# Ten of twelve modulation vectors as row dot products on VectorE in place of fp32 products on TensorE, in a two-layer trunk step

## The chip, the cores and the metric

One NeuronCore of a Trainium2 chip runs the whole kernel; nothing is shared with other cores. The metric is the device time of one execution in microseconds. Before the change three runs gave 2442.68, 2445.26 and 2446.33 us, median 2445.26. The kernel is fp32 in and out: its large products are split into float32r parts that TensorE takes at full rate, three products for one.

## What is computed

One inference step of a two-layer trunk with D = 1024, on 512 sample tokens and 128 prompt tokens. Each token group has a conditioning vector (`c` and `c_ctx`), and each layer turns it into six modulation vectors with one linear map:

```python
def trunk_layer(x, cond, l, P, rope, ctx):
    mod = (jax.nn.silu(cond) @ P['w_mod'][l] + P['b_mod'][l])[:, None, :]
    sh1, sc1, g1, sh2, sc2, g2 = jnp.split(mod, 6, axis=-1)
    h = rmsnorm(x) * (1.0 + sc1) + sh1
    mix, ctx_out = token_mixer(h, l, P, rope, ctx)
    x = x + g1 * mix
    h = rmsnorm(x) * (1.0 + sc2) + sh2
    u = dwconv3(h @ P['w_up'][l], P['ffn_conv_w'][l], P['ffn_conv_b'][l])
    x = x + g2 * ((jax.nn.silu(u[..., :D_FF]) * u[..., D_FF:]) @ P['w_down'][l])
    return x, ctx_out
```

`token_mixer` runs one input projection whose columns feed three branches: a chunked spatial-gating MLP, a chunkwise mLSTM and a differential attention. Each is projected to 1024 columns, multiplied by its sigmoid gate and summed, and one output projection follows. `w_mod` is [2, 1024, 6144] in fp32. The two groups of tokens share all weights and differ in the modulation vectors, so the vectors are needed for two conditionings. Two layers and six vectors make the twelve of the title.

## The kernel before

Features lie on the 128 partitions, tokens on the free axis: an activation is eight tiles of 128x640. A product with a 128-column tile of weights has eight steps of k, three terms each (high by high, high by low, low by high) and two halves of 320 tokens, 48 matmuls of line 129. The weights for it come as one chunk of 128x1024 (512 KB) through the tag `raw`, a ring of three slots in SBUF. `weights` (lines 90 to 103) loads a chunk and splits it: ScalarE writes the high part of 512 columns (line 100), VectorE and GpSimd in turns subtract it for the low part (line 101). All transfers of the kernel are issued by SP, in one order, and a transfer that needs a slot waits for those who still read that slot; the transfers behind it wait too. `acc` and `ms` are the PSUM accumulators, two of each.

A tile scheduler sets the order on each engine when the kernel is built. It works through the program with a model of the engines, and what results is a fixed sequence for each engine with semaphore waits between them; `keep_in_program_order` pins single instructions, `high_priority` moves a piece forward.

A layer runs like this: the spatial gating, the mLSTM's and the attention's heads, with the output tiles of the branches between the heads (`branch`: for each output tile m a gate product of 48 matmuls, then a half product of 24 with `w_branch`, then an accumulation by VectorE in line 897 or 899), last the attention branch, whose first five gates are made ahead (`AHEAD`). Then come `w_out` and, in `handoff`, the next norm: the last two tiles of a product and the first two of the next are cut into token halves, so that VectorE and ScalarE norm one half while TensorE works on the other. The FFN (`ffn`) makes two `w_up` tiles for each of 22 f, convolves them on VectorE out of the accumulator (lines 165 and 167), and sums with `w_down` in three parts of f.

Modulation vectors are made in half vectors of 512 columns. `mod_products` (from line 250) loads `w_mod` in eight tiles of 128x512 (line 259), and TensorE multiplies eight times a 32-column stationary `cs`, the silu of the conditionings padded with zeros, by 512 columns of fp32, four products side by side in column groups of the array (line 264). A copy (line 269), four transposes (line 277), a reduction over the four groups (line 281) and the bias (lines 285 and 287) follow. The first two vectors of layer 0 are made in `start` in quarters of 256 columns. `mod_step` does the next half vector of a list: within the attention branch after each output tile but the first, and in the FFN after f = 2 and 4 and after odd tiles of `w_down`. Its tiles have tags of their own (`wk`, `y`, `mw`) and not `raw`.

## Time and profile before

| | |
|---|---|
| median of the runs | 2445.26 us (2442.68 to 2446.33) |
| span of the profiled execution | 2439.1 us |
| what lies around that span, to the median | 6 us |
| granted TensorE clock, mean | 0.998 |
| bytes moved by DMA | 227 MB, 93 GB/s in the mean |

The profile is one execution. Its times count from the start of the span. TensorE (PE) is the busy engine; its weight loads (PEld) run beside the matmuls. DVE is VectorE, ACT ScalarE, POOL GpSimd. SP only issues transfers. The chain of work that ended last is followed back from the last instruction, at each step to what released it or to what ran before it on its engine.

### The profile page before, as it was taken

How to read it: one execution, taken by the hardware profiler on the slowest of the kernel's cores; microseconds unless marked ns; L12 is line 12 of the kernel's file. 1: busy time of each engine (PE TensorE's matmuls, PEld its weight loads, DVE VectorE, ACT ScalarE, POOL GpSimd, SP SyncE). 2: the span in 40 equal slices, each digit the busy share in tenths (PEclk: the TensorE clock that was granted, in tenths of full speed). 3: DMA queues.
4: the chain of work that ended last, by engine and by line, in shares of the span. 5: the costliest groups of instructions: out<-in, count | busy, mean ns of one | idle time of the engine just before them, and what ended most of it. 6: DMA issues, size and time to landing. Idle time of an engine off the chain costs nothing.

```text
span 2439.1 us, 40662 instructions
## 1 busy us (share of the span) xinstructions
PE 2408.0 (99%) x16708; PEld 2313.9 (95%) x16708; DVE 1134.0 (46%) x2111; ACT 944.8 (39%) x1728; POOL 669.9 (27%) x486
## 2 busy tenths in 40 slices
PE   8999999999999999999999999999999999999998
PEld 7999999999598999999999999999986989999998
DVE  5455545553146433424446455455532454244344
ACT  4433335544145322323454332455442543232334
POOL 2322232332222322313213222323322223232231
PEclk9999999999999999999999999999999999999999
DMA  8221221123544234222322212211233432222222
GB/s 282 74 73 64 65 78 62 60 72 132 173 147 160 69 109 140 72 75 79 103 80 70 74 64 66 76 54 62 97 114 120 147 96 74 79 74 73 81 72 69
DMA packets 88761, 227.39 MB, mean 93 GB/s; under 512 B 9472, under 2 KB 23936, under 8 KB 88576
## 3 DMA queue, kind: packets, MB, share of 16 engines
q1 hardware_dynamic: 88576, 224.80, 28.2%
q8 instruction: 131, 2.15, 0.4%
q14 instruction: 54, 0.44, 0.1%
HBM read 217.41 MB, written 7.35 MB: 92 GB/s over the span
## 4 chain that ended last, share of the span: by engine, by line
PE 96%; DVE 3%; ACT 1%; DMA 0%; issue 0%; SPq 0%; DVEq 0%; POOL 0%; POOLq 0%; ACTq 0%
PE acc L129 77%; PE acc L156 6%; PE ms L264 3%; PE ms L869 2%; PE ms L840 2%; PE ms L156 1%; PE ms L862 1%; PE ms L716 1%; PE ms L718 1%; PE ms L705 1%; DVE x L439 0%; PE ms L670 0%; PE ms L536 0%; PE ms L277 0%; PE ms L327 0%
## 5 line engine op out<-in xcount | busy, mean ns | idle before, releaser
L129 PE MATMUL acc<-h,whi 128*128 128x320 f32 x6464 | 1246.9, 311 | 5.0 <-DVE h L356 3.3
L129 PEld LDWEIGHTS acc<-h,whi 128*128 128x128 f32 x6464 | 1019.3, 188 | 32.1 <-issue 19.3
L100 ACT CAST whi<-raw 128x512 fp32r<-128x512 f32 x596 | 365.3, 614 | 1038.1 <-PE acc L129 787.9
L101 POOL TENSOR_TENSOR wlo<-raw,whi 128x512 fp32r<-128x512 f32 (+1 forms) x298 | 390.7, 1311 | 1355.1 <-ACT whi L100 1304.7
L129 PE MATMUL acc<-h,wlo 128*128 128x320 f32 x3232 | 755.4, 310 | 0.0
L129 PEld LDWEIGHTS acc<-h,wlo 128*128 128x128 f32 x3232 | 544.2, 188 | 3.5 <-issue 3.4
L101 DVE TENSOR_TENSOR wlo<-raw,whi 128x512 fp32r<-128x512 f32 (+1 forms) x298 | 241.2, 810 | 451.0 <-ACT whi L100 435.0
L129 PE MATMUL acc<-act,whi 128*128 128x320 f32 x1408 | 269.6, 310 | 0.0
L129 PEld LDWEIGHTS acc<-act,whi 128*128 128x128 f32 x1408 | 222.0, 188 | 4.2 <-issue 2.5
L129 PE MATMUL acc<-act,wlo 128*128 128x320 f32 x704 | 165.5, 309 | 0.0
L129 PE MATMUL acc<-y,whi 128*128 128x320 f32 x768 | 154.3, 314 | 1.7 <-DVE y L114 1.7
L499 DVE SCALAR_TENSOR_TENSOR x<-acc,mod,x 128x128 f32<-128x128 f32 (+3 forms) x136 | 66.3, 527 | 181.3 <-PE acc L129 181.3
L165 DVE SCALAR_TENSOR_TENSOR cw<-acc,vec,cw 128x511 f32<-128x511 f32 (+1 forms) x176 | 95.7, 544 | 115.1 <-ACT cw L163 114.0
L156 PE MATMUL acc<-whi,h 128*128 128x256 f32 x768 | 145.7, 283 | 0.0
L129 PEld LDWEIGHTS acc<-y,whi 128*128 128x128 f32 x768 | 121.2, 188 | 17.3 <-issue 11.7
L156 PEld LDWEIGHTS acc<-whi,h 128*128 128x128 f32 x768 | 123.0, 192 | 0.0
L129 PEld LDWEIGHTS acc<-act,wlo 128*128 128x128 f32 x704 | 119.1, 188 | 0.0
L916 POOL TENSOR_TENSOR cw<-cw,cw 128x640 f32<-128x640 f32 x44 | 69.2, 1573 | 156.5 <-DVE cw L167 151.9
L156 PE MATMUL acc<-wlo,h 128*128 128x256 f32 x384 | 108.7, 283 | 0.0
L167 DVE SCALAR_TENSOR_TENSOR cw<-acc,vec,cw 128x511 f32<-128x511 f32 (+1 forms) x176 | 96.7, 550 | 6.0
L129 PE MATMUL acc<-y,wlo 128*128 128x320 f32 x384 | 92.1, 315 | 0.0
L848 ACT ACTIVATE wk<-ms,mx 128x640 f32<-128x640 f32 (+1 forms) x80 | 56.7, 709 | 76.6 <-DVE mx L846 73.2
(257 smaller groups left out, 2425.0 us busy)
## 6 DMA issues: line engine op xcount, KB each, us to landing
raw<-w_in_f SPq DMA_DIRECT2D x98, 512.0 KB, 3.4
raw<-w_up SPq DMA_DIRECT2D x88, 512.0 KB, 3.3
wk<-w_mod SPq DMA_DIRECT2D x72, 256.0 KB, 3.4
mw<-w_mod SPq DMA_DIRECT2D x72, 256.0 KB, 5.7
raw<-w_down SPq DMA_DIRECT2D x32, 448.0 KB, 3.3
raw<-w_in_v SPq DMA_DIRECT2D x24, 512.0 KB, 3.7
raw<-w_branch SPq DMA_DIRECT2D x24, 512.0 KB, 3.3
mw<-w_mod SPq DMA_DIRECT2D x16, 512.0 KB, 8.8
```

What stands on the lines that cost most here:

```text
L100: nc.scalar.copy(hi, raw[:, a:b])
L101: self.alt().tensor_sub(lo, raw[:, a:b], hi.bitcast(F32))
L129: ins = nc.tensor.matmul(acc[:, s], a[:, sl], b[:, s], start=k == 0 and i == 0, stop=k == last and i == 2)
L156: nc.tensor.matmul(accs[b], a[:, bs], w[:, sl], start=first and b % 2 == 0, stop=last and (b % 2 == 1 or b == NB - 1))
L165: nc.vector.scalar_tensor_tensor(dst[:, a + 1 : b], acc[:, a : b - 1], w0, dst[:, a + 1 : b], ALU.mult, ALU.add)
L167: nc.vector.scalar_tensor_tensor(dst[:, a : b - 1], acc[:, a + 1 : b], w2, dst[:, a : b - 1], ALU.mult, ALU.add)
L264: ins = nc.tensor.matmul(ps[j : j + 32, 0:width], self.cs[:, k, :], raws[k], start=k < 4, stop=k >= 4, tile_position=(0, j))
L499: self.nc.vector.scalar_tensor_tensor(x[:, a:b], acc[:, a:b], g[:, k, i : i + 1], x[:, a:b], ALU.mult, ALU.add)
L840: nc.tensor.matmul(ps[:, s : s + 320], st[:, qs], kk[:, s : s + 320], start=i == 0, stop=i == 1)
L848: nc.scalar.activation(e[:, 0:nk], ps[:, 0:nk], AF.Exp, bias=mx, scale=scale, accum_out=sm[:, j : j + 1])
L869: nc.tensor.matmul(po, at[:, c * P : (c + 1) * P], vv, start=c == 0, stop=c == n - 1)
L916: nc.gpsimd.tensor_mul(cs[0], cs[0], cs[1])
```

## The change

The two vectors that `start` needs at once stay as they are. The other ten are computed as rows of a transposed `w_mod`: the array `w_modT` holds, for each layer and section, 16 blocks of 64 features with 1024 inputs each. `late_consts` now builds `cb`, a 128x1024 tile with silu of `c` on the lower 64 partitions and of `c_ctx` on the upper ones: two transfers that repeat one row on 64 partitions, a tanh on ScalarE, one operation on VectorE. A `mod_step` takes a slot of `raw`, loads the same block of 64 rows twice, once to each half of the partitions (line 306), and lets VectorE multiply it with `cb` and sum along the row (line 307). Sixteen steps make a vector; then four copies of 64x8 bring the sums into the layout that the norms read, and the bias is added. There are 160 steps. `branch` calls two of them after each output tile of all three branches, so 48 a layer; the FFN calls four after each f below 4, two after the others and one after each part, until the list is empty. The sections move with it: 2 is now made in the gating branch's tiles, 3 in the mLSTM's, 4 in the attention's, and 5 with the next layer's 0 and 1 in the FFN.

```diff
+    def conditionings(self, cp):
...
+        self.cb = self.t(cp, [P, D], F32, "cb")
+        for g in range(2):
+            nc.sync.dma_start(self.cb[64 * g : 64 * g + 64, :], I["cB"][g : g + 1].broadcast_to([64, D]))
+        th = self.t(self.wp, [P, D], F32, "raw")
+        nc.scalar.activation(th, self.cb, AF.Tanh, scale=0.5)
+        nc.vector.scalar_tensor_tensor(self.cb, th, 1.0, self.cb, ALU.add, ALU.mult)
...
-    def mod_step(self, src, pin=False):
-        if self.mod_todo:
-            l, sec, n = self.mod_todo.pop(0)
-            self.mod_part(l, sec, 512 * n, 512, src, pin)
+    def mod_step(self):
+        if not self.mod_todo:
+            return
+        nc = self.nc
+        l, sec, k = self.mod_todo.pop(0)
+        if k == 0:
+            self.mod_raw = self.t(self.mp, [P, KD, 2], F32, "modraw", 2)
+        w = self.t(self.wp, [P, D], F32, "raw")
+        for g in range(2):
+            nc.sync.dma_start(w[64 * g : 64 * g + 64, :], self.I["w_modT"][l, sec * 2 * KD + k])
+        nc.vector.scalar_tensor_tensor(w, w, 0.5, self.cb, ALU.mult, ALU.mult,
+                                       accum_out=self.mod_raw[:, k // 2, k % 2 : k % 2 + 1])
+        if k == 2 * KD - 1:
+            m = self.mods[l, sec] = self.t(self.mp, [P, KD, 2], F32, f"mod{sec}", 2)
+            for g in range(2):
+                for i in range(2):
+                    nc.vector.tensor_copy(m[64 * i : 64 * i + 64, :, g], self.mod_raw[64 * g : 64 * g + 64, :, i])
+            c = V_BMOD + sec * KD
+            b = self.vecs[l][:, c : c + KD].unsqueeze(2).to_broadcast([P, KD, 2])
...
     def branch(self, l, n, h, ys, merged, ms, first=False, last=False, ahead=None):
...
             if last:
                 out.append(self.split(merged[m], self.hp, "h", scale=0.5))
-                if m:
-                    self.mod_step((p, "wk", 1), pin=True)
+            self.mod_step()
+            self.mod_step()
...
             for f in range(len(acts), min(f1 + 1, NF)):
                 up(f)
-                if f in (2, 4):
-                    self.mod_step((p2, "mw", 1))
+                for _ in range(4 if f < 4 else 2):
+                    self.mod_step()
+            self.mod_step()
...
-                elif m % 2:
-                    self.mod_step((p2, "mw", 1))
...
-                    self.mod_todo = [(l, s, n) for s in (2, 3, 4) for n in range(2)][1 if l else 0 :]
+                    self.mod_todo = [(l, s, k) for s in (2, 3, 4) for k in range(2 * KD)]
...
-                    self.mod_todo = [(l, 5, 0), (l, 5, 1)]
-                    if nxt:
-                        self.mod_todo += [(l + 1, s, n) for s in (0, 1) for n in range(2)] + [(l + 1, 2, 0)]
+                    self.mod_todo = [(l + s // 6, s % 6, k) for s in ((5, 6, 7) if nxt else (5,)) for k in range(2 * KD)]
```

Three places show how the sequences change. The number behind a tile's name tells tiles of one tag apart; lines after 207 stand some 10 to 30 further down in the changed file.

SP's queue ahead of the attention branch's tiles in layer 0. Before, behind three chunks of `w_branch`: the last two of eight `w_mod` tiles, which go to slots of their own (`wk`), a table, the weights of gates 5 and 6, and the first two of eight more tiles:

```order
L259 DMA wk_6459<-w_mod 128x512
L259 DMA wk_6461<-w_mod 128x512
L224 DMA lc_12635<-rope 128x512
L94 DMA raw_6695<-w_in_f 128x1024
L94 DMA raw_6820<-w_in_f 128x1024
L259 DMA wk_6522<-w_mod 128x512
L259 DMA wk_6524<-w_mod 128x512
```

After the change, from behind the chunk of `w_branch` for output tiles 2 and 3, ahead of which four more steps stand (each `w_modT` row is two transfers, and the `w_in_f` chunks are gates 5 and 6):

```order
L306 DMA raw_6619<-w_modT 64x1024 x2
L306 DMA raw_6623<-w_modT 64x1024 x2
L306 DMA raw_6658<-w_modT 64x1024 x2
L234 DMA lc_12631<-rope 128x512
L306 DMA raw_6662<-w_modT 64x1024 x2
L94 DMA raw_6666<-w_branch 128x1024
L306 DMA raw_6707<-w_modT 64x1024 x2
L306 DMA raw_6711<-w_modT 64x1024 x2
L94 DMA raw_6716<-w_in_f 128x1024
L306 DMA raw_6807<-w_modT 64x1024 x2
L306 DMA raw_6811<-w_modT 64x1024 x2
L94 DMA raw_6816<-w_in_f 128x1024
```

The small tiles have gone, and steps that share the ring with the weights stand between the chunks.

VectorE at that place: the y parts are the attention's outputs (line 114), line 899 is the accumulation of an output tile. Before:

```order
L114 SCALAR_TENSOR_TENSOR y_6342<-acc_6335,gains_543,y_6341 128x640
L281 TENSOR_REDUCE mod_1007_6295<-ms_6312 128x8
L114 SCALAR_TENSOR_TENSOR y_6352<-acc_6345,gains_543,y_6351 128x640
L287 TENSOR_TENSOR mod_1007_6295<-mod_1007_6295,vec_7_90 128x8
L114 SCALAR_TENSOR_TENSOR y_6362<-acc_6355,gains_543,y_6361 128x640
L114 SCALAR_TENSOR_TENSOR y_6372<-acc_6365,gains_543,y_6371 128x640
L899 SCALAR_TENSOR_TENSOR qk_6049<-qk_6049,acc_6385 128x640
L899 SCALAR_TENSOR_TENSOR qk_6110<-qk_6110,acc_6416 128x640
```

After the change, where the accumulation is line 927:

```order
L307 SCALAR_TENSOR_TENSOR raw_6662,modraw_6530<-raw_6662,cb_540 128x1024
L114 SCALAR_TENSOR_TENSOR y_6456<-acc_6449,gains_549,y_6455 128x640
L114 SCALAR_TENSOR_TENSOR y_6466<-acc_6459,gains_549,y_6465 128x640
L307 SCALAR_TENSOR_TENSOR raw_6707,modraw_6530<-raw_6707,cb_540 128x1024
L114 SCALAR_TENSOR_TENSOR y_6476<-acc_6469,gains_549,y_6475 128x640
L307 SCALAR_TENSOR_TENSOR raw_6711,modraw_6530<-raw_6711,cb_540 128x1024
L114 SCALAR_TENSOR_TENSOR y_6486<-acc_6479,gains_549,y_6485 128x640
L307 SCALAR_TENSOR_TENSOR raw_6807,modraw_6530<-raw_6807,cb_540 128x1024
L927 SCALAR_TENSOR_TENSOR qk_6197<-qk_6197,acc_6499 128x640
L307 SCALAR_TENSOR_TENSOR raw_6811,modraw_6530<-raw_6811,cb_540 128x1024
L927 SCALAR_TENSOR_TENSOR qk_6258<-qk_6258,acc_6539 128x640
```

Steps have come between the y parts, and one ahead of each of the two accumulations.

SP's queue at the start of the FFN of layer 0, before, from the first chunk of `w_up`:

```order
L94 DMA raw_7661<-w_up 128x1024
L94 DMA raw_7671<-w_up 128x1024
L94 DMA raw_7848<-w_up 128x1024
L94 DMA raw_7913<-w_up 128x1024
L94 DMA raw_7984<-w_up 128x1024
L259 DMA mw_8425<-w_mod 128x512
```

After:

```order
L94 DMA raw_7679<-w_up 128x1024
L94 DMA raw_7689<-w_up 128x1024
L94 DMA raw_7866<-w_up 128x1024
L94 DMA raw_7931<-w_up 128x1024
L306 DMA raw_8002<-w_modT 64x1024 x2
L306 DMA raw_8006<-w_modT 64x1024 x2
L306 DMA raw_8010<-w_modT 64x1024 x2
L306 DMA raw_8014<-w_modT 64x1024 x2
L94 DMA raw_8019<-w_up 128x1024
L94 DMA raw_8084<-w_up 128x1024
L306 DMA raw_8154<-w_modT 64x1024 x2
```

Four steps follow the first four chunks, and four more the next two; before, sixteen `w_mod` tiles of `mw` stood behind the first five.

ScalarE in `start`, before: the last copies of the column products, the last h tiles, then the gelu's table.

```order
L269 COPY ev_445<-ms_436 128x256
L269 COPY ev_460<-ms_451 128x256
L438 ACTIVATE h_470<-x_112,mod_35_206,mod_30_188 128x512
L438 ACTIVATE h_470<-x_112,mod_35_206,mod_30_188 128x128
L438 ACTIVATE h_477<-x_113,mod_35_206,mod_30_188 128x512
L438 ACTIVATE h_477<-x_113,mod_35_206,mod_30_188 128x128
L506 ACT_TABLE_LOAD
```

After:

```order
L275 COPY ev_445<-ms_436 128x256
L275 COPY ev_460<-ms_451 128x256
L211 ACT_TABLE_LOAD
L211 ACTIVATE raw_543<-cb_540 128x1024
L534 ACT_TABLE_LOAD
L534 ACTIVATE warm_579<-ones_78 128x1
L466 ACTIVATE h_470<-x_112,mod_35_206,mod_30_188 128x512
L466 ACTIVATE h_470<-x_112,mod_35_206,mod_30_188 128x128
```

The tanh of `cb` and two table loads have come ahead of these h tiles.

## Rows read from the trace of the kernel before

**Rows 1.** The page, part 1: engine busy us (share) xinstructions.

```profile
PE 2408.0 (99%) x16708; PEld 2313.9 (95%) x16708; DVE 1134.0 (46%) x2111; ACT 944.8 (39%) x1728; POOL 669.9 (27%) x486
```

**Rows 2.** The page, part 4: the chain that ended last, by engine and by line.

```profile
PE 96%; DVE 3%; ACT 1%; DMA 0%; issue 0%; SPq 0%; DVEq 0%; POOL 0%; POOLq 0%; ACTq 0%
PE acc L129 77%; PE acc L156 6%; PE ms L264 3%; PE ms L869 2%; PE ms L840 2%; PE ms L156 1%; PE ms L862 1%; PE ms L716 1%; PE ms L718 1%; PE ms L705 1%; DVE x L439 0%; PE ms L670 0%; PE ms L536 0%; PE ms L277 0%; PE ms L327 0%
```

**Rows 3.** Line 264 by stretch: from:to, length, PE busy, PEld busy, clock, DMA share, GB/s.

```profile
590.00:680.00 90.00, 29.82 (x96) 4.40 (x96) 1.00 0.45 144
680.00:1300.00 620.00, 18.42 (x112) 3.44 (x112) 1.00 0.32 103
...
1800.00:1870.00 70.00, 25.82 (x80) 3.74 (x80) 1.00 0.39 129
1870.00:2440.00 570.00, 6.34 (x32) 1.10 (x32) 0.99 0.26 85
```

**Rows 4.** The chain from 590 to 680, its last row from 735 to 830: start, us, what.

```profile
by line: PE acc L129 60.9%; PE ms L264 31.2%; PE ms L277 2.4%; DVE y L114 2.0%; ACT y L113 1.8%; PE acc L744 0.9%; ACT modev L269 0.7%; issue 0.2%; PE ms L869 0.1%
...
620.78 0.78 PE acc L129 x4
...
773.19 56.95 PE acc L129 x387
```

**Rows 5.** VectorE's groups by form: busy us, mean ns of one, idle before.

```profile
L854 DVE SCALAR_TENSOR_TENSOR wk<-wk,smx,wk 128x640 f32<-128x640 f32 x32 | 28.9, 904 | 24.8 <-ACT wk L853 24.5
...
L899 DVE SCALAR_TENSOR_TENSOR tg<-tg,acc 128x640 f32<-128x640 f32 x26 | 21.2, 816 | 44.0 <-PE acc L129 43.3 <-issue 0.7
...
L846 DVE TENSOR_SCALAR mx<-mx 128x1 f32<-128x1 f32 x80 | 12.1, 151 | 2.0
```

**Rows 6.** Line 101 (weight splits) on VectorE: ns min/median/max, first and last start.

```profile
L101 DVE TENSOR_TENSOR wlo<-raw,whi x298: 545/692/2054, 20.6 to 2413.0; 128x512 fp32r<-128x512 f32 x141, 128x384 fp32r<-128x384 f32 x8
```

**Rows 7.** The page, part 6: DMA issues, KB each, median us to landing.

```profile
raw<-w_in_f SPq DMA_DIRECT2D x98, 512.0 KB, 3.4
...
wk<-w_mod SPq DMA_DIRECT2D x72, 256.0 KB, 3.4
mw<-w_mod SPq DMA_DIRECT2D x72, 256.0 KB, 5.7
```

**Rows 8.** SP's queue at two stretches, in order of time: start us, us, issues.

```profile
572.69 10.21 SPq L94 DMA_DIRECT2D raw<-w_branch  x2
...
754.71 12.10 SPq L259 DMA_DIRECT2D mw<-w_mod  x16
...
772.34 0.80 SPq L259 DMA_DIRECT2D mw<-w_mod  x2
```

**Rows 9.** VectorE at two stretches, in order of time: start us, us, operation.

```profile
688.02 0.82 DVE L899 SCALAR_TENSOR_TENSOR tg<-tg,acc 128x640 f32<-128x640 f32 x1 [0.70 <-PE acc L129]
...
748.10 0.68 DVE L101 TENSOR_TENSOR wlo<-raw,whi 128x512 fp32r<-128x512 f32 x1
...
769.15 0.75 DVE L165 SCALAR_TENSOR_TENSOR cw<-acc,vec,cw 128x511 f32<-128x511 f32 x1 [1.97 <-ACT cw L163]
```

**Rows 10.** ScalarE at the start, in order of time: start us, us, operation.

```profile
41.49 0.37 ACT L269 COPY ev<-ms 128x256 f32<-128x256 f32 x1 [0.49 <-PE ms L264]
42.98 2.29 ACT L438 ACTIVATE h<-x,mod,mod 128x512 fp32r<-128x512 f32 x4 [1.11 <-DVE mod L287]
45.29 1.28 ACT L506 ACT_TABLE_LOAD   x1
```

**Rows 11.** Line 218, the load of sg_wT: ns, first and last start, us to landing.

```profile
L218 SPq DMA_DIRECT2D lc<-sg_wT x2: 328/380/432, 32.9 to 529.7; - x2
...
DMA to landing us min/median/max: 6.8/6.8/6.8
```

**Rows 12.** All engines by stretch at the start; PEclk is the granted clock.

```profile
10.00:14.00 4.00, 0.26 (x3) 0.07 (x1) 3.58 (x5) 3.52 (x5) 0.00 (x0) 1.00 1.06 386
14.00:18.00 4.00, 3.82 (x24) 3.82 (x25) 0.32 (x2) 0.61 (x2) 0.00 (x0) 0.70 1.08 402
```

More of the change, by code (lines that the diff above doesn't have):

```diff
@@ L179, in consts @@
         nc.vector.memset(self.eps, EPS)
+    def conditionings(self, cp):
+        nc, I = self.nc, self.I
         ct = self.t(cp, [P, KD, 2], F32, "ct")
@@ L244, in lambdas @@
         nc.vector.tensor_scalar(self.lam, s[:, 0:1], s[:, 1:2], self.lam_init, ALU.subtract, ALU.add)
-    def mod_part(self, l, sec, c0, width, src, pin=False):
-        self.mod_vector(*self.mod_products(l, sec, c0, width, src, pin))
     def mod_products(self, l, sec, c0, width, src, pin=False):
@@ L258, in mod_products @@
             r = self.t(pool, [P, per, width], F32, tag)
-            nc.sync.dma_start(r, self.I["w_mod"][l, sec * 2 + c0 // 512, :, k : k + per, c0 % 512 : c0 % 512 + width])
+            nc.sync.dma_start(r, self.I["w_mod0"][sec * 2 + c0 // 512, :, k : k + per, c0 % 512 : c0 % 512 + width])
             raws += [r[:, i, :] for i in range(per)]
@@ L287, in mod_vector @@
             nc.vector.tensor_add(m, m, b)
-    def mod_step(self, src, pin=False):
-        if self.mod_todo:
-            l, sec, n = self.mod_todo.pop(0)
-            self.mod_part(l, sec, 512 * n, 512, src, pin)
+    def mod_step(self):
[17 more added lines that the diff above has]
+            b = self.vecs[l][:, c : c + KD].unsqueeze(2).to_broadcast([P, KD, 2])
+            if sec in (1, 4):
+                nc.vector.scalar_tensor_tensor(m, m, 1.0, b, ALU.add, ALU.add)
+            else:
+                nc.vector.tensor_add(m, m, b)
     def norm_open(self, l, sec, pool, tag):
@@ L384, in start @@
         nc, pin = self.nc, self.tc.keep_in_program_order
+        self.conditionings(p0)
         x = [self.t(p0, [P, NT], F32, "x") for _ in range(KD)]
@@ L981, in run @@
                     with tc.tile_pool(name="p0", bufs=1, reuse_waits="tile") as p0:
-                        h, accs = self.start(Tags(p0, {"x": 8, "mw": 16, "sq": 2, "sqa": 2, "ev": 2}))
+                        h, accs = self.start(Tags(p0, {"x": 8, "mw": 16, "sq": 2, "sqa": 2, "ev": 2, "ct": 1, "cth": 1, "cs": 1}))
                     self.late_consts()
@@ L1012, in run @@
                     ahead = {m: self.gate(l, G_DA, m, h, t) for m, t in enumerate(AHEAD)}
-                    self.mod_step((self.p1, "y", 1), pin=True)
                     ys = self.attn_out(os, dsums)
@@ L1016, in run @@
                 with tc.tile_pool(name=f"p2{l}", bufs=1, reuse_waits="tile") as p2:
-                    tags = Tags(p2, {"x": 8, "cw": 8, "act": 20, "mw": 8, "sq": 2, "sqa": 2})
+                    tags = Tags(p2, {"x": 8, "cw": 8, "act": 20, "sq": 2, "sqa": 2})
                     x = [self.t(tags, [P, NT], F32, "x") for _ in range(KD)]
@@ L1082, in _layout @@
     A["final_g"] = f["final_g"].reshape(KD, P).T
-    A["w_mod"] = f["w_mod"].reshape(L, KD, P, 12, 512).transpose(0, 3, 2, 1, 4)
+    wm = f["w_mod"]
+    A["w_mod0"] = wm[0, :, : 2 * D].reshape(KD, P, 4, 512).transpose(2, 1, 0, 3)
+    A["w_modT"] = wm.transpose(0, 2, 1).reshape(L, 12 * KD, 64, D)
+    A["cB"] = np.stack([f["c"][0], f["c_ctx"]], 0)
     w = f["w_in"]
```

## Prediction

> **What bounds the kernel now.** I read the page first: TensorE is busy 2408.0 of 2439.1 us, VectorE 1134.0, less than half [rows 1]. The chain of work that ended last says the same from the other side: 96% of it is TensorE, 77% the split products of line 129, 3% the modulation products of line 264 [rows 2]. So an operation taken off TensorE shortens the run by its length as long as TensorE's next products are ready, and one put on VectorE costs nothing until TensorE waits for it. Where the modulation products stand is read from their busy time by stretch [rows 3]: four stretches, of which 590 to 680 and 1800 to 1870 (the attention branch of either layer) hold the most. Then I looked into those stretches with the chain [rows 4] and at the places where the change puts its new work: the queue of transfers, VectorE's sequence, ScalarE's at the start.
>
> The measured runs have a median of 2445.3 us and the profiled execution has a span of 2439.1, so I add 6 us for what lies around the span. One run can be told from no change here at about 0.2%, 4.9 us.
>
> **What leaves TensorE.** From 590 to 680, lines 264 and 277 hold 31.2% and 2.4% of 90 us of the chain [rows 4]: 30 us. The products go in pairs between groups of line 129, and a group of four then takes 0.78 us [rows 4] where four cost 0.59 in a long row (56.95 us for 387 [rows 4]); with some 22 such groups that is 4 more. So 34 us for six half vectors. Layer 1's stretch has 25.82 us of busy products for 29.82 [rows 3], by the same ratio 30. The FFN of layer 0 has seven halves, 18.42 busy [rows 3] and with the transposes, in the ratio above, 20. Layer 1's FFN has two, 6.34 [rows 3], taken as 6, since one of them waits in part. **Gross gain 34 + 30 + 20 + 6 = 90 us.** The copies, reductions and DMAs that go with them hang off the chain.
>
> **What comes, per step.** There are 160 steps, each two transfers of 256 KB and one VectorE operation of 128x1024 with a sum. The trace has no such operation. Its nearest are 128x640 with one operand in PSUM at 816 ns and with both in SBUF at 904 [rows 5]; scaled to 1024 columns 1.31 and 1.45 us. What writing a sum adds is unknown: zero to the 0.15 of the smallest operation [rows 5], and below zero there is no reason for it to go. Against that, an operation with two SBUF operands can last much longer when GpSimd works: line 101 has a median of 0.69 and a maximum of 2.05 [rows 6]. I take 1.4, the row of the same kind, with 1.3 and 2.6 as ends. 160 x 1.4 = 224 us, VectorE at some 55%: that sum alone bounds nothing.
>
> Landing: 512 KB in one transfer take 3.4 us, 256 KB alone 3.4, and 5.7 where eight and more stand in a queue [rows 7]. Sixteen of 256 KB are taken off in 12.10 us, 0.76 each [rows 8]. So two at once should land 3.4 + 0.76 = 4.2 us after the first is issued; the ends are 3.8 (the second issue, 0.40 [rows 8], and then as one of 512 KB) and 6.8 (one after the other). None of the rows is a transfer to 64 partitions only. A step that has to wait for its slot of the ring therefore takes 4.2 + 1.4 = **5.6 us** from issue to issue (5.1 to 8).
>
> The Trainium skill speaks against this layout: the page "SBUF — State Buffer", section "Can I just issue two DMAs to hit both halves?", says that two transfers to different partition halves do not run side by side, and the section on the port swizzle above it gives 196 GB/s to 64 partitions against 328 to 128. No row here shows such a transfer; by an estimate from the page's 2 us and 196 GB/s a step would land after 4.7 us, and the sum below would come out near 2437.
>
> **Where steps are serial.** The ring `raw` has three slots and the weights use it too, and SP issues in order. In the mLSTM's and the gating's output tiles two steps and one and a half weight chunks stand against 10.6 us of TensorE work; there I see at least 4 us of slack and charge 3 us a layer for VectorE's chains that wait behind a step, 0 to 10.
>
> *Attention branch.* The order has twelve steps ahead of the weights of gate tile 6 in SP's queue. Three of them go beside another; nine follow each other slot by slot, since each waits for VectorE to be through with the one before it. From 573 (where the branch weights of tiles 2 and 3 are issued now [rows 8]) nine take 50 us, to 623. VectorE's sequence has the twelfth step ahead of the accumulation of tile 1 (line 899 now, 927 then), and with two accumulators TensorE can be one tile ahead at most. So at 625 there are left five half products of 3.5 us and three gate products of 7.1, 39 us: the last accumulation at 664. Today it starts at 688.0 [rows 9]; without modulation products it would be 688 - 34 = 654. So 10 us are given back, and in layer 1, whose stretch is shorter by 4 while the steps are as many, about 12. Sum 22, and nine more a layer for each us of the step. (A product of 48 takes 7.1 by 56.95 us for 387 [rows 4].)
>
> *Start of the FFN.* Four steps come behind the last w_out and first w_up chunks, one slot, and their VectorE operations stand inside the norm of the second half of tokens, the fourth ahead of the convolution that frees the first accumulator, at 769.15 now [rows 9]. First issue 749, after the split of the second w_up chunk at 748.10 [rows 9]: 749 + 4 x 5.6 = 771.4, then the convolution, so the next product starts near 773. Now it starts at 773.19 [rows 4], after 9 us of modulation work. All 9 go. The two groups after it have four steps and two chunks against 14.1 us; three steps in a row and a chunk make about 17.5: 3.5 each. So 16 us a layer, 32, ten more per us of the step and layer. From f = 4 there are two steps against 14.1 us, and I charge nothing.
>
> *Start.* ScalarE now gets a table load, the tanh of the 128x1024 conditionings, and the gelu's table before the last h tiles, which start at 42.98 [rows 10]. The copy before them ends at 41.9. Table 1.28, tanh 1.8 (by the 2.29 us for 1280 columns), table 1.28 [rows 10]: 46.3, 3.3 us late, and TensorE has little else by then. The conditionings have to be there: the load in that place now, sg_wT, is issued at 32.9 and lands 6.8 us later [rows 11], at 39.7, so 41 with 512 KB more, in time. I charge 3 us, 2 to 8.
>
> **Sum.** 90 - 6 - 22 - 32 - 3 = 27 us. 2439 - 27 + 6 = **2418 us.** With a slope of 38 us for each us of the step (18 in the attention branches, 20 in the FFN) the gain is gone at 6.3 us. A stall of some 4 us can also cost clock: after the idle stretch of 10 to 14 us the granted clock shows 0.70 for 4 us [rows 12], the lower level for most of them. At two places that would be 3 us; it is within the range.
>
> **Rivals.** (a) *Hidden.* VectorE and the queue keep ahead, because the scheduler's waits end earlier than I think or the step lands in 3.8: 5.1 us a step gives 2399, and with nothing lost 2439 - 90 + 6 = 2355. For it: DMA is busy 45% of that stretch [rows 3], SP is free. Against: three slots for weights and steps. 0.22 for 2355 to 2404. (b) *The halves land one after the other*, 4.8 us (between 4.2 and 6.8, nearer to the two together), 6.2 a step: 4 us left, 2441, 2432 to 2450. The page named above says so; no row bears it out or refutes it. 0.14. (c) *VectorE's operation is the long one.* Beside GpSimd's half of the weight splits it lasts 2.6 instead of 1.4: 6.8 us a step and 2464, and every chain behind a step is longer too. It decides from 2.1 us on. For it: line 101's maximum [rows 6]; against it the medians. Slower. 0.22. (d) *The change does not take the products away*: the order has 196 fewer TensorE rows, so no.
>
> **How the numbers follow.** The forecast, 2404 to 2432, gets 0.42. Faster by over 0.2% (under 2440): 0.42 + 0.22 and 0.06 of (b), 0.70. Within 0.2%: 0.08 of (b). Slower: 0.22. The range that leaves out 0.08 below and 0.12 above is 2370 to 2462.
>
> **What will show it.** The new VectorE operation at 1.3 to 1.5 us and its two loads landing at about 4.2 confirm the step; 1.9 and more or 4.8 and more say (c) or (b). The chain of 570 to 670 should carry some 5% of waits for DMA or that operation, ending near 664. The next product after the second half's norm should start later, relative to the norm, than now. In the first 60 us TensorE should wait 3 us for h. I am wrong if the waits lie elsewhere (the mLSTM and attention heads), if the new loads delay weights where I saw slack, or if none of these places shows a wait at all.

## The result

The changed kernel takes 2583.07 us in the median (2579.81 to 2591.53, four runs) against 2445.44 for the kernel before beside it: a ratio of 1.0573, interval 1.0554 to 1.0592. It is 138 us slower; the forecast was 27 us faster, with an end of 2462. The profiled execution has a span of 2577.7 us.

The page of the changed kernel, parts 1, 2, 5 and 6: engine busy us (share), the granted clock in 40 slices, groups (busy us, mean ns of one, idle before and its releaser), DMA issues (KB, median us to landing).

```profile
PE 2393.6 (93%) x16308; PEld 2350.7 (91%) x16308; DVE 1333.6 (52%) x2433; ACT 934.9 (36%) x1719; POOL 689.0 (27%) x486
...
PEclk8999999899898999999999999999998989999999
...
L129 PE MATMUL acc<-h,whi 128*128 128x320 f32 x6464 | 1280.2, 316 | 76.8 <-DVE cw L167 40.6
...
L307 DVE SCALAR_TENSOR_TENSOR raw<-raw,cb 128x1024 f32<-128x1024 f32 x160 | 218.6, 1367 | 385.6 <-DMA raw<-w_modT 376.0
...
raw<-w_modT SPq DMA_DIRECT2D x320, 256.0 KB, 4.0
```

Against [rows 1], TensorE's share has gone from 99 to 93%, with 400 matmuls fewer. VectorE is at 52%, so its load is not the bound. The row to stop at is L307: the new operation takes 1.37 us in the mean, and ahead of it VectorE stood idle for 385.6 us in sum, 376.0 of them waiting for its own load. The row of L129 shows the other end of it: TensorE waits for L167, a convolution on VectorE that has nothing to do with modulation.

The waits of the changed kernel, TensorE's: who waits for whom, us in total, times, longest.

```profile
PE acc L129 <- DVE cw L167: 40.6, 19, 4.3
PE acc L129 <- DVE qk L167: 29.2, 16, 2.9
PE acc L129 <- DVE h L383: 15.9, 15, 2.8
PE acc L772 <- DVE y L114: 14.8, 2, 7.5
PE ms L868 <- ACT osq L900: 11.3, 6, 3.6
PE acc L772 <- DVE hs L767: 7.8, 2, 4.0
```

None of these rows names `raw`, a load or line 307; further down the list the new work stands only with the bias of a finished vector (lines 317 and 319, 4.3 us in three places). So TensorE waits for old work, most of it VectorE's, that stands behind the new. Two stretches show how. First the FFN of layer 0, VectorE in order of time (start us, us, operation, [idle before, releaser]):

```profile
861.53 2.54 DVE L307 SCALAR_TENSOR_TENSOR raw<-raw,cb 128x1024 f32<-128x1024 f32 x1 [2.61 <-DMA raw<-w_modT]
...
864.00 1.77 DVE L101 TENSOR_TENSOR wlo<-raw,whi 128x512 fp32r<-128x512 f32 x1
865.69 0.74 DVE L165 SCALAR_TENSOR_TENSOR cw<-acc,vec,cw 128x511 f32<-128x511 f32 x1
866.47 0.75 DVE L167 SCALAR_TENSOR_TENSOR cw<-acc,vec,cw 128x511 f32<-128x511 f32 x1
867.13 0.34 DVE L165 SCALAR_TENSOR_TENSOR cw<-acc,vec,cw 128x127 f32<-128x127 f32 x1
868.74 1.23 DVE L307 SCALAR_TENSOR_TENSOR raw<-raw,cb 128x1024 f32<-128x1024 f32 x1 [1.26 <-DMA raw<-w_modT]
869.88 0.08 DVE L307 DVE_READ_ACCUMULATOR raw<-raw,cb 128x1 f32 x1
869.88 0.35 DVE L167 SCALAR_TENSOR_TENSOR cw<-acc,vec,cw 128x127 f32<-128x127 f32 x1
```

A convolution is four pieces, two long and two short, and only the last one frees the accumulator. Here a step stands between the third piece and the fourth: VectorE waits 1.26 us for the step's load, computes for 1.23, then does the 0.35 us that TensorE needs. Of the 160 steps 34 stand between pieces of a convolution, like this one. TensorE in the same stretch, then the granted clock around it (from:to, length, PE, PEld, DVE, ACT, POOL busy, clock, DMA share, GB/s), with the attention branch of layer 0 below:

```profile
870.38 0.84 PE L129 MATMUL acc<-h,whi 128*128 128x320 f32 x4 [3.60 <-DVE cw L167]
```

```profile
866.00:870.50 4.50, 0.90 (x7) 0.67 (x6) 2.94 (x6) 0.17 (x1) 0.00 (x0) 1.00 0.72 208
871.00:874.50 3.50, 3.50 (x16) 3.50 (x15) 2.73 (x5) 1.35 (x3) 0.00 (x0) 0.51 0.67 218
875.00:880.00 5.00, 5.00 (x36) 5.00 (x35) 3.08 (x6) 2.43 (x4) 1.66 (x2) 1.00 0.25 65
...
650.00:656.00 6.00, 6.00 (x43) 5.90 (x41) 1.29 (x3) 0.00 (x0) 0.00 (x0) 1.00 0.40 112
...
660.00:680.00 20.00, 9.62 (x37) 8.48 (x38) 13.69 (x16) 4.92 (x6) 5.11 (x3) 0.50 0.72 190
```

TensorE stood for 3.60 us, and for 3.5 us after it the granted clock is 0.51, the lower level: 16 matmuls where the next 5 us hold 36. The stall is paid once as idle time and once more in clock. In the attention branch 20 us pass at 0.50 around stalls of 4.0, 7.3 and 2.3 us. TensorE there, then VectorE:

```profile
660.15 1.30 PE L772 MATMUL acc<-ident,hs 128*128 128x128 f32 x5 [3.98 <-DVE hs L767]
...
670.65 2.40 PE L772 MATMUL acc<-ident,hs 128*128 128x128 f32 x10 [7.34 <-DVE y L114]
675.38 1.44 PE L129 MATMUL acc<-y,whi 128*128 128x320 f32 x4 [2.33 <-DVE y L114]
```

```profile
659.17 2.62 DVE L767 TENSOR_TENSOR hs<-hs,dasum 128x640 f32<-128x640 f32 x2
661.72 2.27 DVE L307 SCALAR_TENSOR_TENSOR raw<-raw,cb 128x1024 f32<-128x1024 f32 x1
...
663.92 2.27 DVE L307 SCALAR_TENSOR_TENSOR raw<-raw,cb 128x1024 f32<-128x1024 f32 x1
...
668.56 1.23 DVE L307 SCALAR_TENSOR_TENSOR raw<-raw,cb 128x1024 f32<-128x1024 f32 x1 [1.76 <-DMA raw<-w_modT]
...
669.71 1.67 DVE L114 SCALAR_TENSOR_TENSOR y<-acc,gains,y 128x640 fp32r<-128x640 f32 x2
```

Three steps stand ahead of the y parts that free the accumulators; TensorE resumes at 670.65, 7.34 us after it stopped. Of this stall only 1.76 us are a wait for a load; two of the operations last 2.27 us here instead of 1.23.

**The balance.** Line 129 has 12960 matmuls in either kernel, so the time at which the n-th of them starts, after less before, says where time is lost. What TensorE no longer does is read from the kernel without loads below, whose dot products had all run before product 2400: from there on it gains 34.9 and 28.6 us in the two attention branches and 19.0 and 2.9 in the two FFNs, 85 us. "Lost" is what each stage gives back of that.

| stage (products) | gross gain | net, after less before | lost | lost, predicted |
|---|---|---|---|---|
| start (to 240) | 0 | +8.4 | 8.4 | 3 |
| gating and mLSTM, layer 0 (to 2400) | 0 | +46.9 | 46.9 | 3 |
| attention, layer 0 (to 2880) | 34.9 | -15.0 | 19.9 | 10 |
| FFN, layer 0 (to 6240) | 19.0 | +41.6 | 60.6 | 16 |
| gating and mLSTM, layer 1 (to 8880) | 0 | +49.8 | 49.8 | 3 |
| attention, layer 1 (to 9360) | 28.6 | -11.3 | 17.3 | 12 |
| FFN, layer 1 (to 10320) | 2.9 | +18.0 | 20.9 | 16 |
| sum | 85.4 | +138.4 | 223.8 | 63 |

A second count, from TensorE's records, agrees. Its idle stretches of more than 0.8 us are 67 with 156.6 us (before: 10 with 13.5), and the stretches at the lower clock level sum to 179.8 us (before: 12.3). 143 us more of idle and half of 168 more at the lower level make 227, against 224 lost.

### The profile page after: what moved, and what is told of

Its sections match the earlier page's. It is cut to its first block, busy times and chain, and to the rows that moved or that the text cites. A ratio compares the mean times of both kernels' runs of the same rounds, so it can differ in the third digit from the quotient of the medians.

```text
span 2577.7 us, 40471 instructions
## 1 busy us (share of the span) xinstructions
PE 2393.6 (93%) x16308; PEld 2350.7 (91%) x16308; DVE 1333.6 (52%) x2433; ACT 934.9 (36%) x1719; POOL 689.0 (27%) x486
## 5 line engine op out<-in xcount | busy, mean ns | idle before, releaser
L129 PE MATMUL acc<-h,whi 128*128 128x320 f32 x6464 | 1280.2, 316 | 76.8 <-DVE cw L167 40.6
L129 PEld LDWEIGHTS acc<-h,whi 128*128 128x128 f32 x6464 | 1044.1, 192 | 94.1 <-issue 53.7
L101 POOL TENSOR_TENSOR wlo<-raw,whi 128x512 fp32r<-128x512 f32 (+1 forms) x298 | 404.8, 1359 | 1355.9 <-ACT whi L100 1345.1
L129 PE MATMUL acc<-h,wlo 128*128 128x320 f32 x3232 | 767.1, 314 | 0.0
L129 PEld LDWEIGHTS acc<-h,wlo 128*128 128x128 f32 x3232 | 557.5, 192 | 0.4
L307 DVE SCALAR_TENSOR_TENSOR raw<-raw,cb 128x1024 f32<-128x1024 f32 x160 | 218.6, 1367 | 385.6 <-DMA raw<-w_modT 376.0
L129 PE MATMUL acc<-act,whi 128*128 128x320 f32 x1408 | 268.3, 309 | 0.0
L129 PEld LDWEIGHTS acc<-act,whi 128*128 128x128 f32 x1408 | 222.1, 188 | 0.0
L129 PE MATMUL acc<-y,whi 128*128 128x320 f32 x768 | 161.7, 330 | 25.6 <-DVE qk L167 19.8
L129 PE MATMUL acc<-act,wlo 128*128 128x320 f32 x704 | 165.6, 309 | 0.0
L129 PEld LDWEIGHTS acc<-y,whi 128*128 128x128 f32 x768 | 131.0, 203 | 29.0 <-issue 21.6
L129 PEld LDWEIGHTS acc<-act,wlo 128*128 128x128 f32 x704 | 119.0, 188 | 0.0
L167 DVE SCALAR_TENSOR_TENSOR cw<-acc,vec,cw 128x511 f32<-128x511 f32 (+1 forms) x176 | 96.6, 549 | 5.0
L129 PE MATMUL acc<-y,wlo 128*128 128x320 f32 x384 | 95.5, 327 | 0.0
```

Source lines behind the costliest of these rows:

```text
L101: self.alt().tensor_sub(lo, raw[:, a:b], hi.bitcast(F32))
L129: ins = nc.tensor.matmul(acc[:, s], a[:, sl], b[:, s], start=k == 0 and i == 0, stop=k == last and i == 2)
L167: nc.vector.scalar_tensor_tensor(dst[:, a : b - 1], acc[:, a + 1 : b], w2, dst[:, a : b - 1], ALU.mult, ALU.add)
L307: nc.vector.scalar_tensor_tensor(w, w, 0.5, self.cb, ALU.mult, ALU.mult, accum_out=self.mod_raw[:, k // 2, k % 2 : k % 2 + 1])
```

## The experiments

Three theories of the loss. *Wait*: VectorE, which works in order, stands at a step until its load lands, and TensorE's next products hang on what stands behind it. *Work*: the 1.4 us of a step in front of that are enough. *Ring*: the steps' loads take slots and queue places from the weights. The first three runs take one of the three away or leave one alone. In the changed kernel *wait* and *ring* hang together: at the 139 steps that VectorE waited for, the load was issued 2.2 us before VectorE stood there (median) and took 4.61 us to land, and ahead of the loads SP had itself waited, for what earlier users of the ring had still to do (us in total, times, longest):

```profile
SPq L306 <- DVE wlo L101: 168.7, 59, 10.1
...
SPq L306 <- DVE raw L307: 104.2, 66, 3.3
```

So the ring sets how early a load starts, and the landing how long it takes from there. The table gives for each the time of the kernel (one run each where no interval stands below) and the loss by stages as above, with the idle time over 0.8 us and the time at the lower clock level (g+m: gating and mLSTM; att: attention).

| kernel | us | start | g+m 0 | att 0 | FFN 0 | g+m 1 | att 1 | FFN 1 | lost | idle | low clock |
|---|---|---|---|---|---|---|---|---|---|---|---|
| after | 2583.1 | 8.4 | 46.9 | 19.9 | 60.6 | 49.8 | 17.3 | 20.9 | 224 | 156.6 | 179.8 |
| e1, no loads, free order | 2431.5 | 23.2 | 50.0 | 0 | 0 | 1.6 | 0 | 0 | 75 | 52.0 | 98.0 |
| e2, loads and free dots | 2455.3 | 22.4 | 56.1 | 1.0 | 9.5 | 5.2 | 0 | 5.1 | 99 | 69.0 | 105.6 |
| e3, 8 columns | 2492.8 | 7.6 | 29.8 | 15.2 | 27.0 | 29.1 | 13.6 | 14.0 | 136 | 102.2 | 131.4 |
| e4, one load | 2419.2 | 9.4 | 3.8 | 15.1 | 15.9 | 3.2 | 10.1 | 5.4 | 63 | 49.8 | 72.5 |
| e5, no loads, kept in order | 2400.4 | 9.4 | 1.4 | 13.2 | 4.3 | 3.0 | 11.7 | 1.4 | 44 | 37.0 | 60.4 |
| e6, two wide loads | 2451.3 | 9.4 | 10.6 | 16.0 | 26.0 | 9.1 | 13.2 | 11.3 | 96 | 70.4 | 90.6 |
| e7, late silu | 2425.3 | 11.5 | 6.6 | 13.6 | 16.5 | 3.9 | 11.5 | 5.8 | 69 | 52.8 | 78.1 |
| e8, spread | 2444.6 | 11.7 | 25.9 | 7.5 | 4.7 | 28.3 | 6.3 | 1.8 | 86 | 65.8 | 88.6 |
| e10, FFN ahead | 2499.1 | 7.6 | 43.6 | 19.9 | 7.0 | 43.9 | 16.5 | 4.2 | 143 | 110.7 | 114.1 |
| e9, fewer crowds | 2401.3 | 10.0 | 4.6 | 8.8 | 8.8 | 4.9 | 8.2 | 2.1 | 47 | 38.6 | 56.4 |

In every row the idle time above 13.5 us and half of the low clock time above 12.3 add up to within 12 us of the loss: stalls of TensorE and the clock that follows them account for the loss. Of the times expected before the runs, those of e6, e8 and e9 came out (the landing in e6 apart, 3.49 us for 3.8); e4 ended 61 us below the range for *wait*, e10 11 us below it and e7 above both of its values; e1, e2, e3 and e5 fell between the values of two theories.

**Work without loads.** The dot products read the resident `cb`.

```diff
-        w = self.t(self.wp, [P, D], F32, "raw")
-        for g in range(2):
-            nc.sync.dma_start(w[64 * g : 64 * g + 64, :], self.I["w_modT"][l, sec * 2 * KD + k])
-        nc.vector.scalar_tensor_tensor(w, w, 0.5, self.cb, ALU.mult, ALU.mult,
+        nc.vector.scalar_tensor_tensor(self.cb, self.cb, 0.0, self.cb, ALU.mult, ALU.mult,
```

> Leaves out the 320 loads of w_modT: the 160 dot products read the resident conditionings, times zero, so ten modulation vectors hold only their bias. Three theories. WAIT: VectorE takes its operations in order and stands at each dot product until its load has landed (376 us in the changed kernel's profile), and what stands behind it keeps TensorE waiting. RING: the loads take slots of the weight ring and weights come late. WORK: 160 dot products of 1.37 us are too much VectorE work. WAIT and RING both expect about 2365 us (2445 less the 90 us of products, a few back), WORK expects 2500 or more.

2431.52 us. With nothing to wait for, the scheduler put all 160 between 50 and 419 us of the span, so the run says nothing on *work* in its place. It gives the gross gain, though, since nothing is left after 419; and it shows that 160 dense operations in 369 us hold TensorE up by some 73 us themselves, the start with the tanh of `cb` included.

**Loads and free dots.** As above, with the loads kept in their slots of `raw` and read by nobody.

```diff
-        nc.vector.scalar_tensor_tensor(w, w, 0.5, self.cb, ALU.mult, ALU.mult,
+        nc.vector.scalar_tensor_tensor(self.cb, self.cb, 0.0, self.cb, ALU.mult, ALU.mult,
```

> Does all loads through the ring and all dot products, but the products read the resident conditionings (times zero) and wait for no load; the vectors hold only their bias. WAIT expects about 2370 us, with TensorE's waits for VectorE gone; RING expects 2480 or more, with the weight splits waiting for their loads; WORK 2500 or more.

2455.27 us. Behind product 2400 the loads cost 21 us in sum where the loads with their dots cost 169. Here VectorE does not have to be through before a slot is free, so this is *ring* without its link to VectorE: that part is small.

**Wait without work.** Load, slot and wait as in the change, the operation over 8 columns instead of 1024.

```diff
-        nc.vector.scalar_tensor_tensor(w, w, 0.5, self.cb, ALU.mult, ALU.mult,
+        nc.vector.scalar_tensor_tensor(w[:, 0:8], w[:, 0:8], 0.5, self.cb[:, 0:8], ALU.mult, ALU.mult,
```

> Does all loads, and the dot products wait for them but sum only the first 8 of 1024 columns, so the vectors are wrong: the wait without the work. WAIT expects 2500 to 2560 us, since the 2.4 us of waiting per step stay and 1.2 of work go; WORK expects about 2380; RING 2500 or more.

2492.81 us, still 48 us slower than before. The row of line 307 in that kernel (ns min/median/max, first and last start; idle before it):

```profile
L307 DVE SCALAR_TENSOR_TENSOR raw<-raw,cb x160: 157/168/1572, 148.6 to 2078.5; 128x8 f32<-128x8 f32 x160
...
  DMA raw<-w_modT: 449.2, 153
```

At 0.17 us a step instead of 1.23, VectorE waits longer for the loads, 449 us, and TensorE loses 136 of the 224 us. Waiting, with next to no work, makes the kernel slower than before. The order did not stay quite the same: 6 of these steps stand between pieces of a convolution, against 34 in the change.

**Work without waits.** No loads, the dots kept in the order of the program.

```diff
...
+        self.tc.keep_in_program_order(
+            nc.vector.scalar_tensor_tensor(self.cb, self.cb, 0.0, self.cb, ALU.mult, ALU.mult,
+                                           accum_out=self.mod_raw[:, k // 2, k % 2 : k % 2 + 1]))
```

> Leaves out the loads of w_modT, as e1 did, but keeps each dot product behind the VectorE operations that stand before it in the program, so the 160 stay spread over the two layers (in e1 they all ran in the first 424 us); they read the resident conditionings, times zero, and the vectors hold only their bias. WAIT (the wait for the loads is what costs) expects 2370 us, that is before less 86 us of products and 10 back; WORK (the dots themselves) expects 2430 or more.

2400.41 us, 45 faster than before. It loses 44 us: 9 at the start, where no step runs yet, 25 in the attention branches, next to nothing in gating, mLSTM and FFN. These are not the change's places, though: kept in order, a step comes 22 VectorE operations later than there (median, 13 to 49), and only 9 stand between pieces of a convolution. So the 44 us are not the price of the operations where the change has them. Nor do they add up with the 136 of the run before, since both hold the start and neither keeps the order; how the 224 us divide between *wait* and *work* isn't shown. An upper end for *work* comes from the next kernel.

**The landing.** What the wait is made of can be changed without touching VectorE: every row stands twice in `w_modT`, and one transfer of 512 KB fills all partitions.

```diff
-        for g in range(2):
-            nc.sync.dma_start(w[64 * g : 64 * g + 64, :], self.I["w_modT"][l, sec * 2 * KD + k])
+        nc.sync.dma_start(w, self.I["w_modT"][l, sec * 2 * KD + k])
...
+    wt = wm.transpose(0, 2, 1).reshape(L, 12 * KD, 64, D)
+    A["w_modT"] = np.concatenate([wt, wt], 2)
```

> The same sums, but the 64 rows lie twice in w_modT in DRAM, and each step has one transfer of 512 KB to 128 partitions in place of two of 256 KB to 64. Landing falls from 4.0 to about 3.3 us and one issue of 0.5 goes. WAIT expects each wait shorter by about 1 us, and 2480 to 2530 us; if the two halves are not what makes the load late, it stays at 2570 to 2590.

2419.23 us: 164 us less than with the halves, for the same bytes, slots and operations. The load's rows in the changed kernel, then in this one (ns min/median/max of the issue; us to landing; who waited):

```profile
L306 SPq DMA_DIRECT2D raw<-w_modT x320: 465/531/1607, 144.9 to 2161.3; - x160
...
  DVE raw L307: 376.0, 139
...
DMA to landing us min/median/max: 3.2/4.0/5.8
```

```profile
L305 SPq DMA_DIRECT2D raw<-w_modT x160: 327/328/827, 145.8 to 2001.9; - x160
...
  DVE raw L306: 186.2, 133
...
DMA to landing us min/median/max: 3.0/3.2/5.3
```

The 4.0 is over all 320 halves. Taken in pairs, the first half lands 3.56 us after its issue and the second, issued 0.52 later, 4.61 us after the first issue (medians of the steps that VectorE waited for, here and below). One transfer lands after 3.25. So a step's data come 1.36 us earlier, and 161 us of loss go: 118 us for each us, where the prediction's slope was 38. TensorE's waits in this kernel:

```profile
PE acc L771 <- DVE hs L766: 13.2, 2, 7.2
PE acc L129 <- DVE cw L167: 11.5, 10, 1.8
PE acc L129 <- DVE h L382: 9.8, 14, 1.8
...
PE acc L129 <- DVE qk L167: 0.8, 1, 0.8
```

The 40.6 and 29.2 us on convolutions have become 11.5 and 0.8; what is left largest stands in the attention branch (line 771) and at the start. The steps stand where they stood, within 4 VectorE operations, 32 of them between pieces of a convolution, so it is the landing that made the difference and not the order. VectorE still waits 186 us for loads here, so the 63 us that are lost, 54 without the start, are the most that the operations can cost at these places.

**Half partitions or two transfers?** Two transfers as in the change, each to all 128 partitions and half of the columns.

```diff
-            nc.sync.dma_start(w[64 * g : 64 * g + 64, :], self.I["w_modT"][l, sec * 2 * KD + k])
+            nc.sync.dma_start(w[:, 512 * g : 512 * g + 512], self.I["w_modT"][l, sec * 2 * KD + k, :, 512 * g : 512 * g + 512])
...
```

> As e4 (rows twice in DRAM) but again two transfers of 256 KB a step, each to all 128 partitions and 512 columns. HALVES (two transfers to different partition halves do not run side by side) expects the second to land about 3.8 us after the first issue and 2430 to 2460 us; COUNT (two transfers in place of one are what is late) expects 4.6 us as in the changed kernel and 2550 or more.

2451.25 us. In pairs the first lands after 2.59 us and the second 3.49 after the first issue. So of the 1.36 us, 1.12 come from the half partitions and 0.24 from there being two transfers; in time it is 132 us and 32, nearly the same for each us. VectorE's wait for its loads falls with them, from 376.0 us to 220.4 and 186.2. The second issue on SP is part of the 0.24; it wasn't taken apart.

**Wait or work, once more, in the FFN.** The change as it is, halves included, but the FFN's steps have four slots of their own and their dot products run one f later, kept behind what the program has before them. As many bytes and operations; each of the 64 loads is issued at least 7.6 us before its dot product (median 26), and VectorE waits for none.

```diff
-                    self.mod_step()
+                    self.mod_load(p2, "mraw")
...
+                self.mod_dot()
...
```

> The changed kernel with its half loads, and in the branches as it is; in the FFN alone the steps load into four slots of their own, and the dot products of a group come one f later, kept behind the VectorE operations traced before. The work, the loads and their landing stay, the wait goes. By the positions of the products of line 129, the changed kernel lost 59 us in the FFN and norm of layer 0 (from product 3360 to 6240, against the kernel without those products) and 21 in layer 1. WAIT expects 60 to 75 of these 80 to come back: 2510 to 2525 us. WORK, or loads that crowd out the weights, expect no more than 20: 2560 or more.

2499.11 us; the FFNs lose 7.0 and 4.2 us instead of 60.6 and 20.9. TensorE's waits:

```profile
PE acc L129 <- DVE qk L167: 29.8, 16, 3.3
PE acc L780 <- DVE y L114: 14.8, 2, 7.5
...
PE acc L129 <- DVE cw L167: 9.2, 6, 2.0
```

The wait on the FFN's convolutions (`cw`) falls from 40.6 to 9.2, while the mLSTM's (`qk`) and the attention's (`y`), whose steps are as before, stay at 29.8 and 14.8. Loads far enough ahead save the FFN. But the run changes more than the lead: the loads leave the ring, and the dot products come 31 VectorE operations later (median, 20 to 58), so it doesn't tell *wait* from *ring* or from the order. That the landing alone decides, with ring and order as they were, rests on the kernels with one load and with two wide ones, for the FFN as for gating and mLSTM.

**The start.** One load, and the tanh of `cb` moved behind the spatial gating.

```diff
+    def late_silu(self):
...
+        pin(nc.scalar.activation(th, self.cb, AF.Tanh, scale=0.5))
+        pin(nc.vector.scalar_tensor_tensor(self.cb, th, 1.0, self.cb, ALU.add, ALU.mult))
...
```

> As e4, with the tanh and the product that make cb moved behind the spatial gating and kept there, so that ScalarE does not make them ahead of the last h tiles. If the start costs what the two traces show up to the 240th product of line 129 (9 us in e4), 6 to 8 of it come back: 2411 to 2413 us. If the start's loss has another cause (its loads), it stays at 2419.

2425.33 us, a miss: 6 us worse than with one load alone. The loss at the start did not go but moved, to one stall of 7.4 us at 99 us:

```profile
PE acc L129 <- ACT whi L100: 7.4, 1, 7.4
```

The weights that came late are the third chunk of `w_in_f`, issued at 100.43 us where the kernel with one load has it at 76.2. In SP's order a transfer of `cache_kT` had come ahead of it, which waited 38.3 us until a product of the spatial gating had freed its slot (start us, us, issues):

```profile
99.02 0.33 SPq L239 DMA_DIRECT2D lc<-cache_kT  x1
...
100.43 0.33 SPq L94 DMA_DIRECT2D raw<-w_in_f  x1
```

Why the scheduler set them in this order is open.

**Other places for the steps.** The late silu, three steps a tile in gating and mLSTM, none in the attention branch, and the FFN's steps thinned to two or one at a time.

```diff
-            self.mod_step()
-            self.mod_step()
+            for _ in range(0 if last else 3):
+                self.mod_step()
...
+                for _ in range(0 if f < 2 else 2 if f < 4 else 1):
+                    self.mod_step()
...
```

> As e7, with the same 160 steps elsewhere: three after each output tile of the gating and mLSTM branches, none in the attention branch, none at the first f of the FFN, one or two after each w_up product, one after odd w_down tiles. If what e4 still loses are the stalls where steps crowd (19 us in the attention branches, about 10 in the FFNs), 2385 us, 2375 to 2400; if three steps a tile are too many for the gating and mLSTM branches, those lose 20 or more and it stays at 2410 or above.

2444.57 us over ten runs, ratio 0.9993 (0.9983 to 1.0003): no change against before, and 25 us worse than with one load alone. Against the late silu, on which it is built, the FFN's part did as meant (16.5 to 4.7 and 5.8 to 1.8 lost) and the attention's lost half as much, but with a third step a tile the 6.6 and 3.9 us in gating and mLSTM became 25.9 and 28.3. That stretch has room for two steps a tile and not for three.

**A version that beats both.** One load; two steps a tile in gating and mLSTM; in the attention branch from tile 1 on, with the dots queued behind the y parts; the FFN as above; `cb` made early in `start`.

```diff
-            self.mod_step()
-            self.mod_step()
+            if last:
+                with self.tc.issue_after(y_last):
+                    for _ in range((0, 2, 2, 2, 2, 3, 3, 2)[m]):
+                        self.mod_step()
+            else:
+                for _ in range(2):
+                    self.mod_step()
...
```

> As e4 (one load of 512 KB a step), with three places mended: the load of cb and its tanh come ahead of the column products' loads, where ScalarE has finished the squares; in the attention branch no step after tile 0, and the dot products are queued behind the y parts; in the FFN the steps are spread as in e8 (which lost 5 us there in layer 0 where e4 lost 17). Against e4's 2419 I expect 16 us from the FFNs, 5 to 7 from the start and about 10 from the attention branches: 2388 us, 2375 to 2405. If the attention branch's loss is the queue of loads rather than the order on VectorE, its 10 us do not come and it is 2400.

2401.3 us (2398.23 to 2404.41, four runs), ratio 0.9822 (0.9806 to 0.9839): 44 us faster than before, 182 faster than the change. Its groups and TensorE's longest waits:

```profile
PE 2338.3 (97%) x16308; PEld 2308.0 (96%) x16308; DVE 1351.4 (56%) x2433; ACT 935.1 (39%) x1718; POOL 700.1 (29%) x486
...
L300 DVE SCALAR_TENSOR_TENSOR raw<-raw,cb 128x1024 f32<-128x1024 f32 x160 | 219.3, 1374 | 226.8 <-DMA raw<-w_modT 224.1
```

```profile
PE acc L129 <- DVE cw L167: 8.6, 7, 1.7
PE acc L129 <- POOL wlo L101: 8.3, 3, 3.5
PE acc L129 <- DVE h L378: 5.1, 11, 0.8
```

VectorE waits longer for its loads than in the kernel with one load (224.1 us against 186.2), and the kernel is 18 us faster: the attention branches and FFNs lose 28 us instead of 46.5. What counts is which work stands behind the wait, not the sum of the wait. The start, which was to come back, did not (10.0 against 9.4): the first two chunks of `w_in_f` stand behind eleven tiles of `w_mod` in SP's order, issued at 23.5 us, where with one load they stand behind four, issued at 11.3, and TensorE stood 3.9 and 3.5 us at their splits. Why the scheduler put them there is open.

## Why the prediction was wrong

- **Gross gain: right.** Predicted 34 + 30 + 20 + 6 = 90; measured 34.9 + 28.6 + 19.0 + 2.9 = 85.
- **The operation: right.** Predicted 1.4 us; median 1.226, mean 1.367, plus 0.08 for reading the accumulator. Rival (c) is there in part: 27 of the 160 last 1.40 to 2.56 us, and each of these overlaps a GpSimd operation, as only 19 of the other 133 do. The mean rules it out as the cause.
- **The landing: too short by 0.4.** Predicted 4.2, measured 4.61, near rival (b)'s 4.8. The Trainium skill, page "SBUF — State Buffer", section "Can I just issue two DMAs to hit both halves?", says that two transfers to different partition halves do not run side by side. The trace agrees: two halves took 1.36 us longer than the same bytes in one transfer to 128 partitions (4.61 against 3.25), and 1.12 longer than two transfers that each span all partitions. But by the prediction's own sum (b) was worth 2441; it does not explain 2583.
- **"Where steps are serial": the step that failed.** I charged waits where steps follow each other slot by slot, at nine steps of an attention branch and the first groups of an FFN. For gating and mLSTM I counted TensorE time against transfers, saw "at least 4 us of slack" and put 3 us a layer on VectorE's chains; measured 47 and 50. For f from 4 on I charged nothing; of the FFN's 60.6 us in layer 0 some 40 lie there. In that count VectorE's operation appears as 1.4 us of a half empty engine. On an engine that works in order the price of an operation is its own time plus the wait for its operand, and both are charged to everything behind it: 139 of 160 steps waited, 2.7 us each. The weights did come in time: TensorE waited 0.5 us for a split of them. The steps' own loads, issued 2.2 us ahead, did not. The same mistake is in the slope: 38 us per us of step, measured 118.
- **Attention branches: another path, and more.** 22 predicted, 37 lost. In layer 0 the twelve steps ahead of gate 6's weights did follow each other in SP's order, from 628 to 684 us, but TensorE waited for no weight there, and for the accumulation of line 927 only 0.92 us. It stood 13.7 us at `hs` and the y parts (lines 767 and 114) on VectorE, and 20 us went by at the lower clock. In the run without loads, in its other order, the two branches still lost 25 us.
- **Start of the FFN: right at first, then too small.** Up to the second group of products (f = 1) layer 0 lost 8.5 us, with 9 predicted, and 12.3 from there to f = 4, with 7 predicted.
- **Start: just outside its range**, 8.4 for 3, ends 2 to 8; 1.9 of them before the first product. As foreseen, TensorE waits for the last h tiles (3.9 us around 50 us).
- **Clock: mis-sized.** I put 3 us on it, within the range, from [rows 12]. Stalls came at some 60 places instead of two, and 168 us more at the lower level than before cost up to 84 us. The clock mean of the changed kernel is 0.966.
- In the order of the prediction's sum (gross; gating and mLSTM; attention; FFN; start) the runs show 85 - 97 - 37 - 82 - 8 instead of 90 - 6 - 22 - 32 - 3. The last sentence of the prediction named the mLSTM as the place where it would fall. The range missed because the 0 to 10 us of that place was a guess at VectorE's chains, not a count of what stands behind each step in the order.

## What to carry to other kernels

Before moving work to a half idle engine, look at what stands behind it in that engine's sequence, and charge the wait for its operand to all of that, at every place where it stands; the engine's free share says nothing on this. If the work must wait for a transfer, give the transfer slots of its own and a lead of a whole tile, or place the work behind what others wait for, and load it in one transfer over all partitions. Where TensorE is the bound, short stalls cost their length and, in these kernels, half of it to a little over the whole of it again in clock (at most 84 us on 143 in the change, 43 on 39 in e1).

## What the runs showed of the hardware

- Two 256 KB transfers to 64 partitions each, queued one behind the other: the second lands 4.61 us after the first's issue. To 128 partitions each: 3.49. One of 512 KB to 128 partitions: 3.25. The first of either pair lands after 3.56 and 2.59 us.
- A multiply with a row sum over 128x1024 fp32 out of SBUF takes 1.23 us on VectorE, up to 2.56 beside GpSimd work, and the sum comes as an instruction of its own, a read of the accumulator of 0.08 us. The Trainium skill, page "VectorE: DVE Perf Modes", section "Two Vector instructions with no wait between them", counts such an operation as two; the trace agrees.
- After a single stall of 3.60 us the granted clock shows 0.51 for 3.5 us; in [rows 12] it was one idle stretch, the 4 us from 10 to 14, followed by 0.70 for 4 us.
